# Where VectorE scans the fourth group of rows: behind the first tile of the tail, or behind the third

## The chip, the cores and the metric

The kernel runs on one core of a Trainium2 chip. The metric is device time in microseconds (us); each time below is a median of runs. "Ratio" is the mean time of one kernel's runs over that of the kernel before in the same rounds, with a 95% interval; it is not quite the ratio of the medians.

In the views of the profile, DVE is VectorE, ACT is ScalarE, POOL is GpSimd, SP is SyncE and PE is TensorE; a "q" behind one of these names is the engine's sequencer, and L143 is line 143 of the kernel.

## The reference

```python
# x: [8, 2048, 4096] f32, w: [4096, 1] f32
proj = (x @ w).squeeze(-1)                      # 8 x 2048 scores
cm = np.maximum.accumulate(proj, axis=1)        # running maximum
is_record = (proj >= cm).astype(np.float32)
return np.cumsum(is_record, axis=1)             # how many records so far
```

x is 268 MB and is read once. Everything else is small: the load of x sets the pace, and what matters beside it is how soon after the last byte the answer is out.

## The kernel before

Of the 2048 positions, the first 1920 come in four groups (4, 4, 4 and 3 times 128), each group as eight buffers, one for each batch. VectorE multiplies and sums columns 0 to 2815 of a row (a "dot"), GpSimd multiplies the other 1280, and ScalarE sums GpSimd's products. When a group is done, PE transposes its sums into one PSUM tile `ps` of 8 batches by positions, and VectorE makes three instructions over it, the *group scans*: running maximum, comparison, running count.

The last 128 positions are the *tail*: 13 loads, here called tiles one to thirteen. Tiles one to six are 2 MB each, seven to thirteen are smaller pieces. A tail tile's sums are spread by batch ("masked"; GpSimd does this for VectorE's sums of tiles one to six) and PE adds them into `ps`, the tile that group four's scans still read. So PE must not write there before these scans are done.

```python
def scans(cm_, cnt_, src, cm0, cnt0, base=1):
    low = neg.to_broadcast(list(src.shape))
    V.tensor_tensor_scan(out=cm_, data0=src, data1=low, ...)._wait_ge(psr, base)...   # L143
    V.tensor_tensor(out=src, in0=src, in1=cm_, op=ALU.is_ge)...                       # L146
    V.tensor_tensor_scan(out=cnt_, data0=src, ...)...then_inc(cs, 1)                  # L149

# ... PE, at the end of a group: waits for VectorE's and ScalarE's last sums, transposes
def group_rows(r):
    T.wait_ge(fr[B - 1], 2).then_inc(p7, 1)
    # ...

# ... the loads of the tail, on SyncE's queue
for i, (m, c0, c1, _, _) in enumerate(TILES):          # 13 tiles
    d = SY.dma_start(out=xb[:, c0:c1], in_=x[...])     # L199
    # ...
    if i == len(TILES) - 4:                            # ahead of the last three loads
        SY.dma_start(out=out[:, STARTS[-1] : S0], in_=cnt[...])._wait_ge(cs, NG + 1)...  # L210

# ... the tail itself; sums() is VectorE's dot, GpSimd's product and ScalarE's sum of a tile
for i, (m, c0, _, _, p) in enumerate(TILES[: -NP]):    # tiles one to eight
    dv = acc_v[:, i : i + 1]
    sums(i, dv, acc_p[:, m : m + 1])
    if m in (0, EARLY):                                # EARLY = 4
        T.wait_ge(cs, NG + 1 + (m > 0))                # PE: group scans (tail scan) done
    if p:
        by_batch(m, acc_p[:, m : m + 1], rows_of(m)[0] == 0, False, pa, na)
    mm = by_batch(m, dv, False, rows_of(m)[0] + H == B and c0 == 0, sd, nv)
    if m == 0:
        group_scans(RS[-1])
    if m == EARLY - 1:
        mm.then_inc(psr, 1)
    if m == EARLY:
        tail_scans(0, EARLY, ..., 4)                   # first half of the tail
for j in range(NP):                                    # tiles nine to thirteen
    i = len(TILES) - NP + j
    sums(i, accs[:, j : j + 1], accs[:, NP + j : NP + j + 1])
V.wait_ge(pa, na)
V.tensor_reduce(out=fin, in_=accs, ...)                # the "final reduce", L400
# ... mask, matmul, three short scans, output DMA
```

## Time and profile before

| | before |
|---|---|
| time, median of three runs | 633.47 us (633.19 to 633.48) |
| span of the profiled run | 631.3 us |
| rate of the load | 425 GB/s over the span |
| VectorE's wait before the group scans | 4.3 us |
| last tile landed | 624.61 us into the span |
| final reduce starts | 626.88 us |

A *landing* here is the moment at which a load's semaphore got the last of its 16 increments, read from the trace.

From the page of the kernel before, the span, the DMA row of the 40 slices (9 is 90% busy or more) and the bytes:

```profile
span 631.3 us, 1182 instructions
DMA  9999999999999999999999999999999999999994
HBM read 268.45 MB, written 0.07 MB: 425 GB/s over the span
```

The load runs without a hole to the last slice. The Trainium skill ("Perfetto Trace Analysis", section "Roofline") names about 435 GB/s for the 16 DMA engines of a core together; the 425 here agree. So the change is aimed at what comes behind the last landing.

VectorE's waits in the window 595 to 631 us, kernel before (waiter, what it waited for, us in total, times, longest):

```profile
DVE cm L143 <- PE ps L319: 4.3, 1, 4.3
DVE cm_l L143 <- PE ps L373: 0.5, 1, 0.5
DVE small L400 <- ACT xall L133: 0.2, 1, 0.2
```

There is one large wait, before the group scans, and none on a DMA. The timeline of the same stretch (start, duration, engine, line, operation, output and inputs; in brackets the idle time just before, and its releaser), from the group scans to the final reduce:

```profile
601.57 1.00 DVE L143 TENSOR_TENSOR_SCAN cm<-ps,cm,small 8x384 f32<-8x384 f32 x1 [4.29 <-PE ps L319]
602.61 0.55 DVE L146 TENSOR_TENSOR ps<-ps,cm 8x384 f32<-8x384 f32 x1
603.20 1.00 DVE L149 TENSOR_TENSOR_SCAN cnt<-ps,cnt,small 8x384 f32<-8x384 f32 x1
604.13 3.05 DVE L127 CUSTOM_DVE_ANT_0 xall<-xall,w_v 128x2816 f32<-128x2816 f32 x1
...
610.13 3.07 DVE L127 CUSTOM_DVE_ANT_0 xall<-xall,w_v 128x2816 f32<-128x2816 f32 x1
...
617.03 3.05 DVE L127 CUSTOM_DVE_ANT_0 xall<-xall,w_v 128x2816 f32<-128x2816 f32 x1
620.02 1.30 DVE L127 CUSTOM_DVE_ANT_0 xall<-xall,w_v 128x1120 f32<-128x1120 f32 x1
...
626.20 0.50 DVE L127 CUSTOM_DVE_ANT_0 xall<-xall,w_v 128x352 f32<-128x352 f32 x1
626.88 0.16 DVE L400 TENSOR_REDUCE small<-small 128x1 f32<-128x10 f32 x1 [0.17 <-ACT xall L133]
```

No bracket stands between the scans and the final reduce: VectorE works without a pause and never waits for data. The dot at 604.13 is that of tile two, which had landed at 594.92. The chain of waits that ended last, in order of time (start, duration, what), kernel before:

```profile
598.81 2.73 PE ps L319 x12
...
601.57 1.02 DVE cm L143
...
617.10 2.98 DVE xall L127
...
620.17 0.20 POOL masked L357
620.37 2.86 POOL xall L343
...
625.34 1.45 ACT xall L133 x6
```

It runs from PE's transposes through VectorE's dots; from 620.17 it passes over GpSimd, whose product of tile seven stood behind a mask that waited for VectorE, to ScalarE's last sum. Two engines therefore end nearly together: VectorE at 626.7 and ScalarE at 626.8.

### The profile page before, as it was taken

Reading aid. Unit: us, or ns where it says so; the run is one execution under the profiler, and the core shown is the slowest. Engines: PE = TensorE matmul, PEld = TensorE weight load, DVE = VectorE, ACT = ScalarE, POOL = GpSimd, SP = SyncE. Lnnn points to the kernel's source line nnn. Section 1 sums busy time; section 2 is a strip of 40 time slices with the busy share of each in tenths; the row PEclk is TensorE's granted clock in tenths of the full one; section 3 lists DMA queues with packets and bytes.
Section 4 is the critical chain, followed back from the end, with each engine's and each line's share of the span. In section 5 each row is a group of like instructions: output and inputs, shape, how many; then the busy total and the mean of one; then the engine's idle time right before and its main releaser. Section 6 shows DMA issues by size and latency. Waiting matters only on the chain. (4 is left out here: it accounts for less than half of the span.)

```text
span 631.3 us, 1182 instructions
## 1 busy us (share of the span) xinstructions
PE 31.9 (5%) x108; PEld 14.8 (2%) x108; DVE 406.6 (64%) x292; ACT 180.1 (29%) x273; POOL 369.8 (59%) x147
## 2 busy tenths in 40 slices
PE   7100000000010000000020000000002000000021
PEld 3000000000000000000010000000001000000010
DVE  0755676556785557755569655577557966555787
ACT  1222332123322223322233222332222323323244
POOL 0555676445765557755567655577554766665776
PEclk9999999999999999999996555555556555555555
DMA  9999999999999999999999999999999999999994
GB/s 400 399 465 403 461 428 436 429 436 436 428 453 411 457 407 457 408 457 407 461 403 461 403 465 403 462 411 453 432 426 439 415 445 439 412 445 414 429 424 199
DMA packets 6579, 268.55 MB, mean 425 GB/s; under 512 B 768, under 2 KB 1040, under 8 KB 1584
## 3 DMA queue, kind: packets, MB, share of 16 engines
q1 hardware_dynamic: 6560, 268.50, 98.6%
q10 hardware_dynamic: 16, 0.02, 0.0%
q14 instruction: 3, 0.02, 0.0%
HBM read 268.45 MB, written 0.07 MB: 425 GB/s over the span
## 5 line engine op out<-in xcount | busy, mean ns | idle before, releaser
L127 DVE CUSTOM_DVE_ANT_0 xall<-xall,w_v 128x2816 f32<-128x2816 f32 (+3 forms) x133 | 388.2, 2972 | 183.9 <-DMA xall<-in_x_dram 183.9
L287 POOL TENSOR_TENSOR xall<-xall,w_sb 128x1280 f32<-128x1280 f32 x120 | 344.8, 2906 | 250.0 <-POOLq L290 250.0
L133 ACT ACTIVATE xall<-xall 128x1280 f32<-128x1280 f32 (+1 forms) x130 | 162.8, 1252 | 430.6 <-POOL xall L287 415.8
L319 PE MATMUL ps<-identity,small 128*8 128x128 f32 x60 | 13.1, 407 | 570.8 <-PEq L316 570.8
L133 ACT ACTIVATION_READ_ACCUMULATOR xall<-xall 128x1 f32 x130 | 24.2, 186 | 0.0
L343 POOL TENSOR_TENSOR xall<-xall,w_sb 128x1280 f32<-128x1280 f32 (+1 forms) x8 | 21.6, 2704 | 0.0
L319 PEld LDWEIGHTS ps<-identity,small 128*8 128x8 f32 x60 | 7.3, 126 | 577.7 <-issue 573.5
L143 DVE TENSOR_TENSOR_SCAN cm<-ps,cm,small 8x512 f32<-8x512 f32 (+1 forms) x5 | 6.1, 1218 | 18.3 <-PE ps L319 18.3
L231 PE MATMUL w_v<-w,identity 8*128 8x512 f32 x14 | 12.1, 1056 | 0.0
L253 DVE MEMSET ps<- 8x512 f32 x1 | 0.5, 485 | 16.5 <-ACT w L242 16.5
L127 DVE DVE_READ_ACCUMULATOR2_ANT small<- 128x1 f32 x133 | 10.7, 80 | 0.0
L149 DVE TENSOR_TENSOR_SCAN cnt<-ps,cnt,small 8x512 f32<-8x512 f32 (+1 forms) x5 | 6.1, 1217 | 0.2
L373 PE MATMUL ps<-fold,masked 128*8 128x64 f32 x32 | 4.7, 302 | 21.4 <-ACT masked L361 14.7
L231 PEld LDWEIGHTS w_v<-w,identity 8*128 8x128 f32 x14 | 4.6, 332 | 7.3 <-issue 7.3
L357 POOL TENSOR_TENSOR masked<-fold,small 128x8 f32<-128x8 f32 x6 | 1.3, 211 | 5.2 <-DVE small L127 5.2
L239 ACT COPY w_sb<-w_v 128x768 f32<-128x768 f32 x1 | 0.8, 798 | 11.4 <-PE w_v L231 11.4
L146 DVE TENSOR_TENSOR ps<-ps,cm 8x512 f32<-8x512 f32 (+1 forms) x5 | 3.3, 660 | 0.2
L373 PEld LDWEIGHTS ps<-fold,masked 128*8 128x8 f32 x32 | 2.4, 109 | 24.0 <-ACT masked L361 16.1
L361 ACT ACTIVATE masked<-fold,small 128x8 f32<-128x8 f32 x9 | 2.5, 298 | 0.2
L231 PE MATMUL ps<-w,identity 8*128 8x512 f32 x2 | 2.1, 1137 | 3.6 <-DMA w<-in_w_dram 3.6
L238 ACT ACT_TABLE_LOAD x1 | 1.3, 1283 | 2.7 <-DVE fold L249 2.7
L245 DVE TENSOR_REDUCE fold<-identity 128x2 f32<-128x128 f32 x1 | 0.3, 287 | 2.1 <-POOL cnt L224 2.1
(23 smaller groups left out, 7.3 us busy)
## 6 DMA issues: line engine op xcount, KB each, us to landing
xall<-in_x_dram SPq DMA_DIRECT2D x8, 6144.0 KB, 30.5
xall<-in_x_dram SPq DMA_DIRECT2D x6, 2048.0 KB, 39.5
xall<-in_x_dram SPq DMA_DIRECT2D x1, 1200.0 KB, 33.5
xall<-in_x_dram SPq DMA_DIRECT2D x1, 848.0 KB, 35.1
xall<-in_x_dram SPq DMA_DIRECT2D x1, 752.0 KB, 36.3
xall<-in_x_dram SPq DMA_DIRECT2D x1, 576.0 KB, 37.0
xall<-in_x_dram SPq DMA_DIRECT2D x24, 45.0
xall<-in_x_dram SPq DMA_DIRECT2D x1, 352.0 KB, 19.1
```

The lines of the kernel that those rows point to most:

```text
L127: return V.tensor_tensor_reduce(out=xsl, in0=xsl, in1=wsl, scale=1.0, scalar=0.0, op0=ALU.mult, op1=ALU.add, accum_out=dst,)
L133: return A.activation(out=xsl, in_=xsl, func=ACTF.Copy, accum_out=dst)
L143: V.tensor_tensor_scan(out=cm_, data0=src, data1=low, initial=cm0, op0=ALU.max, op1=ALU.max,)._wait_ge(psr, base).then_inc(psr, 1)
L146: V.tensor_tensor(out=src, in0=src, in1=cm_, op=ALU.is_ge)._wait_ge(psr, base + 1).then_inc(psr, 1)
L149: V.tensor_tensor_scan(out=cnt_, data0=src, data1=low, initial=cnt0, op0=ALU.add, op1=ALU.max,)._wait_ge(psr, base + 2).then_inc(cs, 1)
L231: i = T.matmul(out=dst, lhsT=identity[:NW, k : k + 1].to_broadcast([NW, P]), rhs=w_row, start=True, stop=True,).then_inc(bw, 1)
L238: A.copy(out=w_sb[:, CV - VC :], in_=ps)._wait_ge(bw, 1).then_inc(wc, 1)
L287: i = G.tensor_mul(out=xl, in0=xl, in1=w_sb).then_inc(pl, 1)
L319: i = T.matmul(out=ps[:B, j : r * P : r], lhsT=l[:, j * B : (j + 1) * B], rhs=identity, start=k == 0, stop=k == 1,)
L343: G.tensor_mul(out=xl, in0=xl, in1=w_pool(*p))._wait_ge(xq[i], 16).then_inc(pl, 1)
L361: A.activation(out=e, in_=on, func=ACTF.Copy, scale=acc)._wait_ge(*wait).then_inc(ms, 1)
L373: return T.matmul(out=ps[:B, q : q + Q], lhsT=e, rhs=by_i, start=start, stop=bool(stop),)._wait_ge(*((mg, on_g) if pool else (ms, on_a)))
```

## The change

The group scans of group four need PE's transposes, which need ScalarE's last sum of the group. The change lets VectorE do two more dots first. No instruction is added or removed; on VectorE three instructions move, on the other engines the order stays.

```diff
             mm = by_batch(m, dv, False, rows_of(m)[0] + H == B and c0 == 0, sd, nv)
-            if m == 0:
+            if i == 2:
                 group_scans(RS[-1])
             if m == EARLY - 1:
```

## The prediction

> **What bounds the kernel.** For most of the 631.3 us span it is the load of x: the slices row shows DMA at 0.9 or more in 39 of 40 slices, 425 GB/s on average. (The Trainium skill, "Perfetto Trace Analysis", section "Roofline", puts a core's 16 DMA engines at about 435 GB/s; this trace agrees.) DMA idles only at the end: the stage table shows it stopping between 622 and 624 us of the span, and by issue time plus time to landing the last tile lands at about 624.6 us. What follows is a tail of 6.7 us.
>
> The tail is VectorE's. The waits view shows VectorE stopped for 4.3 us (597.3 to 601.57) before the scan of group four, waiting for PE's transposes (598.8 to 601.5), which wait for ScalarE's last sum. Then come the scans (2.6 us, 601.57 to 604.2) and tile two's dot. From there VectorE runs without a gap to 626.7: it is late, its data is there. Tiles two to seven land at about 594.9, 599.8, 604.7, 609.6, 614.5 and 617.4, but their dots start at 604.1, 607.1, 610.1, 613.1, 617.0 and 620.0.
>
> **What the change does.** Nothing is added or removed. On VectorE the three scan instructions move behind two more dots (3.0 us each). The dots of tiles two and three fill the 4.3 us hole, because both have landed when VectorE gets there (597.2 and 600.2). The scans then run at about 603.3 to 605.9 without waiting, and tile four's dot starts 4.2 us earlier than before, at 605.9.
>
> **How much of it counts.** Not 4.2 us, since VectorE then catches up with the DMA. My schedule with the landing times held: dots at 605.9, 609.7 (waits for data), tail scan 612.7, 614.6 (waits), 617.6, 619.5 (waits), 621.3, 622.75 (waits), 623.7 (waits), 624.3, 624.8, done at about 625.3 instead of 626.7. GpSimd, which was held up by VectorE through its masks (620.17 in the chain of waits), is freed too: its last products then follow the landings (about 621.3, 622.8, 623.7), and ScalarE's last sum ends near 624.9 instead of 626.8. So the final reduce starts about 1.4 us earlier, and the chain behind it (reduce, mask, matmul, three short scans, output DMA) keeps its length.
>
> Costs: SyncE's output of group four waits for the scans, so it and the last three loads of x behind it are issued 1.7 us later, at 606 instead of 604.2. They have 19 us from issue to landing, as they queue behind earlier loads, so they should land when they did. PE's matmuls of the first three tiles start after 605.9 and take some 1.5 us, done well before the tail scan at 612.7 needs tile four's.
>
> **Time.** 633.47 - 1.4 = 632.1 us, range 631.4 to 632.9 (runs scatter by 0.3 us). Chance of faster by over 2%: 0.005; within 2%: 0.99; slower: 0.005.
>
> **What would show the steps.** Right: VectorE's wait on PE before the first scan (4.3 us) gone; scans start near 603.3; new waits of VectorE on DMA before dots of the tail, 3 to 4 us in sum; last landing still near 624.6; final reduce near 625.5; span near 629.9. Wrong: last landing later by about 1.7 us, or the tail scan stopping for PE, or the last reduce still waiting for ScalarE.
>
> **What would make it wrong.** The late output DMA delaying the last loads; the load of x itself drifting by a microsecond, which moves the end as much as the change; GpSimd or ScalarE, slower per tile (3.0 us against 2.9 to 3.1), becoming the last to finish; the chain starting sooner on engines that then collide.

## The result, and the profile after

| | before | after |
|---|---|---|
| time, median of 4 | 633.37 us (633.19 to 633.48) | 631.87 us (631.36 to 632.01) |
| ratio | | 0.9975 [0.9958, 0.9992] |
| span of the profiled run | 631.3 us | 630.0 us |
| last tile landed | 624.61 us | 624.92 us |
| final reduce starts | 626.88 us | 625.65 us |
| from last landing to final reduce | 2.27 us | 0.73 us |

The change saves 1.50 us by the medians, and the interval leaves 1 out. That is far inside 2%.

VectorE's waits in the window 595 to 631 us, kernel after:

```profile
DVE xall L127 <- DMA xall<-in_x_dram: 2.6, 4, 0.9
DVE cm_l L143 <- PE ps L373: 0.5, 1, 0.5
```

The 4.3 us wait on PE is gone, and so is the short one on ScalarE. In their place stand four waits on the load, 2.6 us in all. VectorE's timeline, kernel after:

```profile
600.50 3.08 DVE L127 CUSTOM_DVE_ANT_0 xall<-xall,w_v 128x2816 f32<-128x2816 f32 x1
...
603.51 1.00 DVE L143 TENSOR_TENSOR_SCAN cm<-ps,cm,small 8x384 f32<-8x384 f32 x1
...
606.06 3.05 DVE L127 CUSTOM_DVE_ANT_0 xall<-xall,w_v 128x2816 f32<-128x2816 f32 x1
...
609.94 3.09 DVE L127 CUSTOM_DVE_ANT_0 xall<-xall,w_v 128x2816 f32<-128x2816 f32 x1 [0.82 <-DMA xall<-in_x_dram]
...
614.83 3.09 DVE L127 CUSTOM_DVE_ANT_0 xall<-xall,w_v 128x2816 f32<-128x2816 f32 x1 [0.91 <-DMA xall<-in_x_dram]
...
619.80 1.92 DVE L127 CUSTOM_DVE_ANT_0 xall<-xall,w_v 128x1696 f32<-128x1696 f32 x1 [0.64 <-DMA xall<-in_x_dram]
...
625.65 0.16 DVE L400 TENSOR_REDUCE small<-small 128x1 f32<-128x10 f32 x1
```

The scans start at 603.51 with no bracket: the transposes were done. The dot of tile four starts at 606.06 where it was at 610.13. Then the brackets begin, and each takes back some of the lead:

| dot of tile | start before | start after | lead | that tile's landing, after |
|---|---|---|---|---|
| four | 610.13 | 606.06 | 4.07 | 605.01 |
| five | 613.14 | 609.94 | 3.20 | 609.92 |
| six | 617.03 | 614.83 | 2.20 | 614.80 |
| eight | 621.26 | 619.80 | 1.46 | 619.78 |
| ten | 624.21 | 623.09 | 1.12 | 623.07 |
| thirteen | 626.20 | 625.09 | 1.11 | 624.92 |
| final reduce | 626.88 | 625.65 | 1.23 | |

Four times a dot starts 0.02 or 0.03 us behind its landing: VectorE has caught up with the load. In this profile the landings are 0.3 us later than in that of before, already for tile two (595.23 against 594.92), which is loaded ahead of the change; so it is scatter between executions. Counted from the last landing, the final reduce comes 2.27 - 0.73 = 1.54 us sooner.

The chain of waits that ended last, kernel after:

```profile
586.01 37.06 DMA xall<-in_x_dram
623.07 0.02 issue
623.09 0.99 DVE xall L127
...
625.65 0.17 DVE small L400
```

The chain is now the load of tile ten, issued at 586.01 and landed at 623.07, and then four dots. From 586.01 on GpSimd and ScalarE are off it, and so are PE's transposes.

### The profile page after: what moved, and what is told of

Its sections match the earlier page's. It is cut to its first block, busy times and chain, and to the rows that moved or that the text cites. A ratio compares the mean times of both kernels' runs of the same rounds, so it can differ in the third digit from the quotient of the medians.

```text
span 630.0 us, 1182 instructions
## 1 busy us (share of the span) xinstructions
PE 31.7 (5%) x108; PEld 15.1 (2%) x108; DVE 406.9 (65%) x292; ACT 180.4 (29%) x273; POOL 370.1 (59%) x147
## 4 chain that ended last, share of the span: by engine, by line
POOL 52%; issue 38%; DMA 6%; PE 2%; DVE 1%; SPq 0%; POOLq 0%; ACT 0%; ACTq 0%
POOL xall L287 52%; DMA xall<-in_x_dram 6%; PE w_v L231 2%; PE ps L231 0%; DVE xall L127 0%; SPq L199 0%; DMA w<-in_w_dram 0%; POOLq L290 0%; ACT w L242 0%; PE ps L373 0%; DVE cm_l L143 0%; DVE cnt_l L149 0%; DVE ps L146 0%; ACT xall L133 0%; DVE masked L365 0%
## 5 line engine op out<-in xcount | busy, mean ns | idle before, releaser
L343 POOL TENSOR_TENSOR xall<-xall,w 128x352 f32<-128x352 f32 (+1 forms) x2 | 1.5, 766 | 0.2 <-DMA xall<-in_x_dram 0.2
```

Of the source, the lines that this page charges most:

```text
L343: G.tensor_mul(out=xl, in0=xl, in1=w_pool(*p))._wait_ge(xq[i], 16).then_inc(pl, 1)
```

## The experiments

Theories: **A**: in the kernel before, VectorE is late from the transposes to the end; in the changed one it meets the landings, so a filled hole counts only up to that meeting. **B**: every microsecond of hole filled is worth its share of the gain. **C**: a later scan delays the last loads, which stand behind the output DMA on SyncE's queue, and that costs. **D**: the landings bound the kernel before too. **E**: the gain came through GpSimd, which the change freed from waiting for VectorE.

| run | median us | before, same rounds | ratio, 95% interval | last landing to final reduce, us |
|---|---|---|---|---|
| changed kernel again | 631.70 | 633.21 | 0.9977 [0.9964, 0.9991] | 0.76 |
| scans behind the second tile | 631.72 | 633.21 | 0.9979 [0.9965, 0.9992] | 0.73 |
| behind the fourth | 631.97 | 633.21 | 0.9978 [0.9965, 0.9992] | 0.76 |
| behind the fifth | 634.53 | 633.21 | 1.0022 [1.0008, 1.0036] | 3.44 |
| before, half a tile less | 633.16 | 633.35 | 0.9999 [0.9982, 1.0015] | 4.65 |
| after, half a tile less | 629.22 | 633.35 | 0.9937 [0.9920, 0.9953] | 0.72 |
| before, one instruction more | 634.33 | 633.35 | 1.0019 [1.0002, 1.0035] | 3.55 |
| after, one instruction more | 631.64 | 633.35 | 0.9977 [0.9960, 0.9993] | 0.75 |
| before, masks on ScalarE | 633.18 | 633.18 | 0.9999 [0.9986, 1.0013] | 2.12 |
| after, last loads issued first | 631.53 | 633.18 | 0.9972 [0.9959, 0.9986] | 0.77 |
| after, 96 columns moved | 631.63 | 633.18 | 0.9975 [0.9961, 0.9988] | 0.66 |

The rows of one block (four, four and three runs) ran on the same chip in the same rounds. All outputs are right.

### The changed kernel again

No edit.

> The changed kernel once more, on the chip of the three runs beside it. Both theories: 1.2 to 1.6 us below the kernel before (about 631.9 us).

It was 1.51 us below the kernel before, by the medians of five and nine runs. The result repeats in new rounds.

### Scans behind the second tile

```diff
-            if i == 2:
+            if i == 1:
```

> Scans behind the second tile's dot. Only 3.0 of the 4.3 us hole are filled: VectorE still waits about 1.3 us for PE before the scan (600.2 to 601.6), and the dots of tiles four and five run 1.2 us and 0.3 us later than in the changed kernel. Theory A (the tail is bound by the landings once VectorE has caught up; a filled hole counts only until then): VectorE still meets the landing of tile six at about 614.6, everything from there is as in the changed kernel, same time within 0.2 us. Rival B (every microsecond of filled hole is worth the same share): 3.0 / 4.3 of the gain, so about 0.45 us slower than the changed kernel, and the final reduce that much later behind the last landing.

VectorE's timeline of this kernel:

```profile
601.76 1.00 DVE L143 TENSOR_TENSOR_SCAN cm<-ps,cm,small 8x384 f32<-8x384 f32 x1 [1.28 <-PE ps L319]
...
610.32 3.07 DVE L127 CUSTOM_DVE_ANT_0 xall<-xall,w_v 128x2816 f32<-128x2816 f32 x1
...
614.73 3.09 DVE L127 CUSTOM_DVE_ANT_0 xall<-xall,w_v 128x2816 f32<-128x2816 f32 x1 [0.45 <-DMA xall<-in_x_dram]
```

A hole of 1.28 us is left, and tile five's dot starts at 610.32, 0.4 us later than in the changed kernel. At tile six VectorE waits for the load all the same (0.45 us, where the changed kernel waited 0.91), and from there the two are alike: 0.73 us from last landing to final reduce in both. B expected this gap 0.45 us longer. The times agree, 631.72 against 631.70, but runs of one kernel scatter by 0.6 us, so the gap is the sharper sign. The last third of the hole was worth nothing that these runs can show.

### Scans behind the fourth tile

```diff
-            if i == 2:
+            if i == 3:
```

> Scans behind the fourth tile's dot. VectorE waits for tile four's landing before the scans instead of behind them (about 1.5 us), scans at about 607.8 to 610.4, tile five's dot at 610.4, tail scan at 613.4, tile six's dot at its landing, 614.5 to 614.8. Theory A: same time as the changed kernel within 0.2 us. Rival B has no hole left to fill either and expects the same; rival C (a later scan delays the last loads of x behind the output DMA on the issuing queue, now issued at about 610.5) expects the last landing about 4 us later and a slower kernel.

VectorE's timeline of this kernel:

```profile
605.17 3.09 DVE L127 CUSTOM_DVE_ANT_0 xall<-xall,w_v 128x2816 f32<-128x2816 f32 x1 [1.44 <-DMA xall<-in_x_dram]
...
608.19 1.00 DVE L143 TENSOR_TENSOR_SCAN cm<-ps,cm,small 8x384 f32<-8x384 f32 x1
...
614.97 3.09 DVE L127 CUSTOM_DVE_ANT_0 xall<-xall,w_v 128x2816 f32<-128x2816 f32 x1 [0.28 <-DMA xall<-in_x_dram]
```

The scans began at 608.19, after a wait of 1.44 us for tile four; tile six's dot still waited for its landing (0.28 us). The last three loads were issued at 611.2 and later and the last one landed at 625.05, 0.1 us behind the changed kernel's 624.92, not 4 us. The time is that of the changed kernel within the scatter: 0.27 us above it by the medians, 0.06 us by the ratios, with the same gap of 0.76 us. C fell for a delay of this size.

### Scans behind the fifth tile

```diff
-            if i == 2:
+            if i == 4:
```

> Scans behind the fifth tile's dot, directly ahead of the tail scan. Theory A: scans at about 612.7 to 615.3, then PE works off its ten held matmuls and the tail scan waits about 1 us for it, tile six's dot starts at about 617.3, where it was in the kernel before (617.0); from there VectorE is late again to the end, so the gain is gone: 0 to 0.5 us slower than the kernel before. Last three loads issued at about 615.5 still land when they did (near 624.7). Rival C: last landing some 9 us later, kernel slower by several microseconds.

VectorE's timeline of this kernel:

```profile
614.34 1.00 DVE L149 TENSOR_TENSOR_SCAN cnt<-ps,cnt,small 8x384 f32<-8x384 f32 x1
617.39 0.34 DVE L143 TENSOR_TENSOR_SCAN cm_l<-ps,cm,small 8x64 f32<-8x64 f32 x1 [2.05 <-PE ps L373]
...
618.29 3.05 DVE L127 CUSTOM_DVE_ANT_0 xall<-xall,w_v 128x2816 f32<-128x2816 f32 x1
```

And PE's:

```profile
615.49 1.87 PE L373 MATMUL ps<-fold,masked 128*8 128x64 f32 x16 [13.86 <-DVE cnt L149]
```

The sign was as expected and the size was not: 1.32 us slower than the kernel before, where 0 to 0.5 were expected. The mis-sized term is PE's catching up. It had to wait for the group scans, and then did the eight matmuls of tiles one to four in 1.87 us, so VectorE waited 2.05 us instead of about 1. The ten held matmuls of the expectation were eight, since those of tile five stand behind the tail scan in PE's order. Each of these matmuls shows as two records; I had read the 8 records of the changed kernel (1.01 us) as 8 matmuls when they were four. With that, tile six's dot starts at 618.29, 1.26 us behind the kernel before, and the end is 1.32 us behind it: late VectorE is paid in full. The last three loads, issued at 615.7 to 617.0, still landed at 624.69. C fell for this delay too.

### Half a tile less to load, in both kernels

The load of tile four brings 2048 of its 4096 columns; the other half keeps old data. The dots are as long as before.

```diff
-                out=xb[:, c0:c1],
+                out=xb[:, c0:c1] if i != 3 else xb[:, : D // 2],
...
-                    S0 + rows_of(m)[1] : S0 + rows_of(m)[1] + Q, c0:c1,
+                    S0 + rows_of(m)[1] : S0 + rows_of(m)[1] + Q,
+                    c0 : c1 if i != 3 else D // 2,
```

> The kernel before, with half of the tail's fourth tile (1 of 2 MB) not loaded; its result is wrong on purpose, its work is the same. Every landing behind it comes about 2.4 us earlier (last one near 622.2). Theory A (the tail of the kernel before is bound by VectorE from the transposes on, not by the landings): VectorE's dots stay where they were (610.1, 613.1, 617.0, 620.0), time unchanged within 0.3 us. Rival D (the landings bound the kernel before too): about 2.4 us faster.

> The changed kernel with the same half tile not loaded (result wrong on purpose). Theory A (the changed kernel's end follows the landings): 1.7 to 2.5 us faster than the changed kernel (near 629.5 us), VectorE's waits on DMA in the tail mostly gone. If the end did not follow the landings: unchanged near 631.8 us.

The last landing came at 622.55 and 622.45 us, some 2.1 to 2.5 us earlier. The kernel before did not move (0.9999): its last dots stand where they stood, now 4 us behind their data. VectorE's timeline of the kernel before with half a tile less:

```profile
626.51 0.50 DVE L127 CUSTOM_DVE_ANT_0 xall<-xall,w_v 128x352 f32<-128x352 f32 x1
627.20 0.16 DVE L401 TENSOR_REDUCE small<-small 128x1 f32<-128x10 f32 x1 [0.17 <-ACT xall L133]
```

And of the changed kernel with half a tile less:

```profile
622.62 0.51 DVE L127 CUSTOM_DVE_ANT_0 xall<-xall,w_v 128x352 f32<-128x352 f32 x1
623.17 0.16 DVE L401 TENSOR_REDUCE small<-small 128x1 f32<-128x10 f32 x1
```

Here the final reduce moved from 625.65 to 623.17, with the landing. The time fell to 629.22, 4.1 us below the kernel before where the changed kernel is 1.5 below it. The changed kernel itself did not run in these rounds; with one instruction more it did, at 631.64 (below), and 629.22 is 2.4 us under that. So the same megabyte less is worth nothing before the change and about 2.5 us after it: D fell, and A's two halves are shown each by its own run. (The results passed, though they were made wrong on purpose. Presumably few scores among the last 128 of 2048 positions make a record; I didn't look into it.)

### One VectorE instruction more, in both kernels

```diff
                 group_scans(RS[-1])
+                V.tensor_reduce(
+                    out=small[:, 340:341], in_=w_v[:, :1152], op=ALU.add,
+                    axis=mybir.AxisListType.X,
+                )
```

> The kernel before with one more VectorE instruction of about 1.2 to 1.3 us directly behind the scans (a sum over 1152 columns that nobody uses). Theory A: VectorE is late from there to the end, so its whole length is paid: 1.2 to 1.3 us slower than the kernel before. Rival D: nearly nothing.

> The changed kernel with the same instruction behind its scans. Theory A: it eats VectorE's waits on DMA (0.8 us before the dot of tile five, 0.9 us before that of tile six) and is gone by tile six: 0 to 0.2 us slower than the changed kernel.

In the kernel before, VectorE's timeline shows the instruction and the next dot:

```profile
603.99 1.32 DVE L392 TENSOR_REDUCE small<-w_v 128x1 f32<-128x1152 f32 x1
605.24 3.07 DVE L127 CUSTOM_DVE_ANT_0 xall<-xall,w_v 128x2816 f32<-128x2816 f32 x1
```

The dot is put off by 605.24 - 603.99 = 1.25 us. From the start of the scans to the final reduce it took 628.01 - 601.43 = 26.58 us, against 626.88 - 601.57 = 25.31 without: 1.27 us, the whole length. The times say 1.0 us by the medians and 1.2 by the ratio. In the changed kernel the instruction is as long, and VectorE's waits on the load fall from 2.6 to 1.4 us:

```profile
DVE xall L127 <- DMA xall<-in_x_dram: 1.4, 3, 0.6
```

The time does not move: ratio 0.9977, as without it.

### The masks on ScalarE, in the kernel before

```diff
-            pool = m < B - 2 and wait[0] is sd
+            pool = False
```

> The kernel before, with the masks that GpSimd makes for VectorE's sums made by ScalarE instead, so that GpSimd never waits for VectorE in the tail. Rival E (the gain of the change came through GpSimd: in the kernel before the chain of waits ran through its mask at 620.2, which held its product of tile seven back by 3 us): about 1.2 us faster, like the changed kernel. Theory A (VectorE by itself ends at 626.7 there, 0.17 us before the reduce could start): GpSimd's products come 3 us earlier, ScalarE's last sum before 626.3, and the time falls by 0 to 0.2 us only.

GpSimd's waits in the window 595 to 633 us of this kernel hold one line, on the load alone:

```profile
POOL xall L343 <- DMA xall<-in_x_dram: 4.5, 4, 2.0
```

Its product of tile seven, at 620.33 before, now runs right behind that of tile six, and ScalarE's last sum ends at 625.06, where it was 626.8:

```profile
624.88 0.19 ACT L133 ACTIVATION_READ_ACCUMULATOR xall<-xall 128x1 f32 x1
...
626.86 0.16 DVE L400 TENSOR_REDUCE small<-small 128x1 f32<-128x10 f32 x1
```

The time stayed: 633.18 against 633.18. VectorE's last dot still ended at 626.8, and the final reduce began at 626.86. E fell: the chain of waits of the kernel before did pass over GpSimd, but VectorE ran along beside it 0.17 us shorter, so freeing GpSimd alone buys no more than 0.15 us (2.12 us from last landing to final reduce, where it was 2.27), too little for the times to show.

### The last loads ahead of the output DMA, in the changed kernel

```diff
-            if i == len(TILES) - 4:
+            if i == len(TILES) - 1:
```

> The changed kernel with the output DMA of group four issued behind the last three loads of x instead of ahead of them. The three loads are then issued near 590 instead of 606.5. If the late issue of these loads cost something (rival C, weak form), their landing would come earlier and the kernel would be faster by up to 1 us. Theory A: they queue behind the same loads, last landing unchanged within 0.3 us (near 624.8), time within 0.2 us of the changed kernel.

The three loads were issued at 590.1, 594.4 and 600.8 (not all near 590: two of these issue instructions ran for 4.2 us and one for 6.4). The last landing was 624.88, as in the changed kernel (624.92), and so was the final reduce, 625.65. The medians, 631.53 here and 631.70 for the changed kernel in other rounds on another chip, differ by 0.17 us in the direction of C's weak form, less than the scatter of either; a cost of the late issue of that size can't be excluded. A cost near the 1 us that was set as its upper end is not there: the landing did not move.

How a late issue can cost nothing shows in the two times of an issue. The DMA view of the source line, last two loads of the kernel before:

```profile
L199 SPq DMA_DIRECT2D xall<-in_x_dram x2: 606/606/606, 605.2 to 605.8; - x2
DMA to landing us min/median/max: 18.8/18.9/19.0
```

And the same two of the kernel after:

```profile
L199 SPq DMA_DIRECT2D xall<-in_x_dram x2: 606/606/606, 607.1 to 607.8; - x2
DMA to landing us min/median/max: 17.2/17.3/17.4
```

The issue takes 0.606 us in both. It came 1.9 us later, and the time to landing is 1.6 us shorter: the loads stood in line behind others, and their turn came when it came before, but for the 0.3 us of scatter. The Trainium skill ("Perfetto Trace Analysis", section "DMA Instruction — HWDGE (DVE, Sync)") says that the record of an issue leaves the movement of the data out; here 0.6 us of record stand against 17 to 19 us to landing.

### 96 columns from VectorE to GpSimd, in the changed kernel

```diff
-        (B - 1, 736, 1440, (736, 1248), (1248, 1440)),
+        (B - 1, 736, 1440, (736, 1152), (1152, 1440)),
...
-    W2, W2C = 1248, 544
+    W2, W2C = 1152, 640
```

> An attempt to beat the changed kernel: 96 columns of the third tile from the end go from VectorE to GpSimd, because VectorE now starts the last two dots 0.14 and 0.17 us behind their landings, while ScalarE's last sum has 0.5 us to spare. Theory A: VectorE's dot before the last starts at its landing, the last one about 0.1 us earlier; at most 0.1 us faster, too little for the times to show, if at all in the gap between last landing and final reduce (0.73 us before).

The gap from last landing to final reduce was 0.66 us, the smallest of all, 0.07 us below that of the changed kernel. The times, 631.63, can't tell the two apart. VectorE's last dot, 0.52 us of this gap, can't start before the last landing, so by my estimate from these two figures, with the loads cut as they are, the stretch up to the final reduce has no more to give than a tenth or two.

## Why the prediction was right

The median, 631.87, lies in the range, 0.2 us from the predicted 632.1, and the saving of 1.50 us is close to the 1.4 forecast (1.54 counted from the last landing). That the two agree to 0.1 us is luck in part, as runs of one kernel scatter by 0.3 to 0.8 us.

- *"The tail is VectorE's"*: right, and shown by two runs. A megabyte less to load left the kernel before unmoved, and 1.25 us more on VectorE were paid.
- *The hole of 4.3 us filled by two dots, scans near 603.3 with no wait*: right, 603.51.
- *"Not 4.2 us, since VectorE then catches up with the DMA"*: right. The lead shrank from 4.07 us at tile four to 1.11 at tile thirteen. The runs behind the second and the fourth tile put it more sharply: a third of the hole left open, or another wait put in, cost nothing.
- *Waits on the load of 3 to 4 us in sum*: too large; 2.6 us. The term was mis-added: the five waits in the prediction's own schedule come to about 2.8 us when the dots are as long as in the profile, and the fifth of them is next to nothing.
- *GpSimd's last products near 621.3, 622.8 and 623.7, ScalarE's last sum near 624.9, final reduce near 625.5, span near 629.9*: measured at 621.68, 623.13 (two in a row), 625.12, 625.65 and 630.0, the landings themselves 0.3 us later than in the profile of before.
- *SyncE's loads issued 1.7 us later, landing unmoved*: issued 1.9 us later; landing later by the 0.3 us that tile two, ahead of the change, shows as well. Issuing them earlier, or 9 us later still, moved the landing by no more than 0.3 us.
- *PE's held matmuls done well before the tail scan needs them*: right here, since the tail scan at 612.96 did not wait. That they can count was shown by the run behind the fifth tile, where VectorE waited 2.05 us for them.

What stays open: whether the late issue of the last loads costs one or two tenths; what makes the landings scatter from execution to execution (that of tile one, ahead of every edit, came between 589.9 and 590.5 us in the 13 profiles); and how much of the gain is left in a kernel whose masks are on ScalarE from the start, which was not run.

## What to carry to other kernels

An engine that is late at the end of a load-bound kernel can be helped by giving it ready work ahead of an instruction that waits, but the help counts only until the engine meets the load; lay the landings beside the schedule and take the smaller of the two gains. That meeting makes a plateau: three places for the scans, behind the second, third and fourth tile, gave the same time. Behind the fifth the kernel was slower: of the 2.7 us that the gap from last landing to final reduce grew against the changed kernel, 2.05 us show as VectorE's wait for PE, which had stood waiting behind the scans. The Trainium skill says ("Perfetto Trace Analysis", section "Optimization Strategy" under "Identifying Performance Opportunities") that the most contended engine can change between regimes of one kernel, and that interleaving the regimes can help beside work within each; here the limit changed from the load to VectorE in the last 30 us of 631, and all of the gain was there.

## What the Trainium skill lacked or had wrong

- "DMA: Bandwidth & Descriptors" has no figure that I found for how many loads can be issued ahead of the DMA engines before an issue instruction itself is held up. With the last loads issued first, the issues of tiles ten to thirteen ran for 4.0, 4.2, 6.4 and 4.2 us, against 0.5 to 0.6 us for the nine before them, and ended at 590.0, 594.3, 600.7 and 605.0 us, each within 1 us of the landing of tiles one, two, three and four (590.3, 595.2, 600.1 and 605.0). That suggests that about nine loads of this kind are taken on ahead. In the kernels before and after, the issue of tile ten ran for 4.0 and 3.7 us.
- The same page, section "Why a DMA increments its semaphore by 16 and not by 1", says that the up to 16 engines of a DMA finish independently, without saying by how much they drift apart. In the changed kernel the last tile's increments came from 623.15 to 624.92 us, 1.8 us for a load of 176 KB; thirteen of the sixteen had come by 623.68, the last three at 624.20, 624.23 and 624.92. In the run with the last loads issued first it was 1.1 us. For a kernel that ends with such a wait this is as large as the whole gain told here.
- No page that I read says that an f32 matmul shows as two records in a trace. Eight matmuls showed as 16 records here (1.87 us), and that halved an estimate.
- No page that I found says how much the granted TensorE clock differs from one execution of a kernel to the next. It was between 0.64 and 0.89 in runs of one kernel whose times agree within 0.6 us (changed kernel: 631.49 us at 0.891, 631.70 at 0.645). With PE busy 5% of the span, no effect on the time shows: the kernel before took 633.19 us in the mean of 15 runs near 0.645 and 633.28 in the mean of 8 near 0.766.
